# Two decoder layers on one core: twelve convolution taps as diagonal matmuls, and the low halves of the memory keys and values taken from PSUM

## The chip, the cores and the metric

The kernel runs on one core of a Trainium2 chip. The metric is device time in microseconds (us) of one execution. The five engines are TensorE (PE), VectorE (DVE), ScalarE (ACT), GpSimd (POOL) and SyncE (SP, which issues DMAs here). Each works through its own list of instructions in order and waits at semaphores for the others.

## The reference, cut to what matters

One inference step of a trunk of two layers, for 512 prompt positions and 8 sample positions, width 1024. Layer 0 mixes with an S5 and an HGRN2 branch, layer 1 with a Conformer convolution; each layer then has cross-attention into 256 memory tokens and a gated feed-forward part.

```
def _causal_dwconv(u, buf, w, b):
    n_tap = w.shape[0]
    ext = jnp.concatenate([buf.astype(u.dtype), u], axis=1)
    out = lax.conv_general_dilated(ext, w.astype(u.dtype)[:, None, :], (1,), 'VALID',
                                   dimension_numbers=('NWC', 'WIO', 'NWC'),
                                   feature_group_count=u.shape[-1])
    return out + b.astype(u.dtype), ext[:, ext.shape[1] - (n_tap - 1):]
...
def _conformer_conv(z, buf, w_dw, b_dw, ln_g, ln_b):
    a, gate = jnp.split(z, 2, axis=-1)
    u = a * jax.nn.sigmoid(gate)
    c, new_buf = _causal_dwconv(u, buf, w_dw, b_dw)
    return jax.nn.silu(_layer_norm(c, ln_g, ln_b)), new_buf
...
def _cross_attn(h, k, v, wq, wo):
    n, l, _ = h.shape
    q = (h @ wq).reshape(n, l, X_HEADS, X_HEAD_DIM)
    s = jnp.einsum('nlhd,nmhd->nhlm', q, k.astype(q.dtype)).astype(jnp.float32) * (X_HEAD_DIM ** -0.5)
```

The convolution has 31 taps on 1024 channels. The keys and values of the prompt's memory (`mem @ w_xk`, `mem @ w_xv`) are outputs too, for each layer.

## The kernel before, in words

Channels lie on the 128 partitions (eight channel tiles), positions along the free dimension: 512 prompt positions (`LP`) and 8 sample ones, in all 520 (`NT`). Norms and projections take the positions in two halves of 256 and 264 columns. A float32 product is made of three matmuls: each operand is split into a high half, rounded by ACT (`whi`, `xnh`, `Kh`, `Vh`), and a low half, the difference, which DVE or POOL subtracts (`wlo`, `xnl`, `Kl`, `Vl`).

The order of each engine's list is set when the kernel is built: a scheduler with a model of time (`schedule_with_timeline_sim`) places the instructions of each engine, and tiles come from pools with a fixed number of buffers. A tile that takes over a buffer waits for all readers of the tile before it there. Two such pools lie in PSUM: psA with three buffers of two banks (`pa`) and psB with two of one bank (`pb`). Weight tiles `wraw` have a ring of three, loaded by DMAs that SP issues.

Memory, layer 0 (`memory_k`, `memory_v`, called while the mixer's output is normed and added to the residual): four groups of 48 matmuls write the keys of two channel tiles each, `pkk`, a tile of psB. `kf` is a copy of it by ACT into SBUF, for the output's DMA; `Kh` is the rounded copy of `kf`, `Kl = kf - Kh`. The values, `pvv`, lie in psA and go the same way through `vf`. On ACT and DVE these stand among the work of the residual and the next norm: `x` adds (line 384), `xnh`, `xnl`, `whi`, `wlo`.

Layer 1 (`mixer1`): per channel tile the gate `cu` is made of two projections (`pca`, `pcg`), then the convolution runs tile by tile (`conv`). `POOL_TAPS` gives the taps that POOL does: ACT scales a shifted copy `ct`, POOL adds it to `cc`; tiles 1 and 4 lie wholly there, and of tile 6 fifteen taps. The other taps are `scalar_tensor_tensor` operations of DVE, in place on a PSUM tile `pcv` of psB, which ACT starts with tap 0 and the bias. The generator `chain` hands out DVE's taps, `CSTEP` (13) of them with each gate. Then `memory_k` and `memory_v` of layer 1 follow, with plain float32 matmuls (lines 1262 and 1293) and `pkk` and `pvv` both in psA, and the LayerNorm's column sums `pcs` over the eight `cc` tiles.

Of the kernel before, what the change touches and what calls it, by code (L numbers as in the profile page):

```python
# [9 lines left out]
F32 = mybir.dt.float32  # L10
F32R = mybir.dt.float32r
I32 = mybir.dt.int32
AF = mybir.ActivationFunctionType
# [5 lines left out]
P = 128  # L19
D = 1024  # L20
KC = D // P
LP = 512
NB = 8
NT = LP + NB
# [16 lines left out]
CPAIR = (1, 3)  # L41
NE = "VG"
LG = ((0, 0, 0), (0, 0, 0), (0, 1, 1))
POOL_TAPS = {1: 31, 4: 31, 6: 15}
CSTEP = 13
FILL = (4, 1, 5, 4)
NSOP = 8
START = (0, (0, 2, 0), 1, (2, 2, 0), (4, 4, 0), 2, (0, 4, 1), (4, 4, 1))
# [7 lines left out]
NM = 256  # L56
# [3 lines left out]
CW = 31  # L60
# [12 lines left out]
def _cols(n):  # L73
    a = _col[0]
    _col[0] += n
    return a
# [8 lines left out]
PC_CB = _cols(KC)  # L85
# [16 lines left out]
def trunk(ctx, tc, I, O, dbg=None):  # L102
    nc = tc.nc
    V, A, G, T = nc.vector, nc.scalar, nc.gpsimd, nc.tensor
# [21 lines left out]
    def pb(name):  # L126
        return psB.tile([P, 512], F32, tag="pb", name=name)

    def act(out, in_, f, **kw):
        return A.activation(out, in_, f, **kw)  # L130
# [5 lines left out]
    def tt(e, out, a, b, op):  # L136
        e.tensor_tensor(out, a, b, op=op)  # L137

    def stt(out, in0, s, in1, op0, op1):
        V.scalar_tensor_tensor(out, in0, s, in1, op0=op0, op1=op1)  # L140
# [7 lines left out]
    MUL, ADD, SUB = ALU.mult, ALU.add, ALU.subtract  # L148

    def f32(t):  # L150
        return t.bitcast(F32)
# [3 lines left out]
    ident = cst[:, 0:128]  # L155
# [14 lines left out]
    def pcol(base, c):  # L170
        return par[:, base + c:base + c + 1]
# [237 lines left out]
    def mixer0(nxt):  # L409
# [28 lines left out]
        with ExitStack() as es:  # L438
# [296 lines left out]
            def s5_emit(hf, Hs, E, other):  # L735
                Y = sop([P, 16, H5], "Y")
                for gq in range(2):
# [3 lines left out]
                    for g4 in range(4):  # L741
# [6 lines left out]
                        for g2 in range(2):  # L748
                            g = 2 * j + g2
                            T.matmul(pv[:, g2, g4, :], TPt[hf][:, g].rearrange("p c t -> p (c t)"), Us[hf, g][:, NB:U5],  # L750
                                     start=False, stop=True)
                        for _ in range(FILL[3] // 2):
                            next(other)
# [97 lines left out]
            in_u(mm(pa("pu"), load_w(I["w_ab_in"][3]), xs))  # L851
            fill(FILL[0])
            s5_u(0)
            s5_u(1)
            M = []
            for hf in range(2):
                M.append(s5_ops(hf))
                s5_rows(hf)
                fill(0 if hf else FILL[1])
            for hf in range(2):  # L860
# [4 lines left out]
            E = [s5_E(hf) for hf in range(2)]  # L865
            fill(FILL[2])
            Hsts, t1, t2 = s5_scan()
# [216 lines left out]
    def mixer1(bd, nxt, kvp, hs, mem):  # L1084
        nrm, xs = bd.nrm, bd.nrm.xs
        l = 1
        with ExitStack() as es:
            cf = es.enter_context(tc.tile_pool(name="cf", bufs=1))
            cw = par[:, PC_CW:PC_CW + CW * KC].rearrange("p (c j) -> p c j", j=CW)

            us, cs = [], [None] * KC
# [14 lines left out]
            def conv(n):  # L1106
                u, np_ = us[n], POOL_TAPS.get(n, 0)
                c = cs[n] = cf.tile([P, NT], F32, tag="cc", name="cc", bufs=KC)
# [13 lines left out]
                if cut:  # L1122
# [11 lines left out]
                        act(c[:, 0:1], pc[:, 0:1], AF.Copy)  # L1134
                    yield

            def chain(ns):
                for n in ns:
                    yield from conv(n)
# [2 lines left out]
            p0 = project_first(xs, bd.ws, RC, nrm, CUTC)  # L1142
            r = nrm.r
            gate(0, *p0[:2])
            dve = chain(n for n in range(KC) if POOL_TAPS.get(n, 0) < CW)
            for n in range(1, KC):
                for _ in range(CSTEP):
                    next(dve)
                pg = p0[2] if n == 1 else mm(pa("pcg"), wl(KC + n), xs)
                pu = mm(pa("pca"), wl(n), xs)  # L1150
                gate(n, pg, pu)
                if POOL_TAPS.get(n, 0) == CW:
                    for _ in conv(n):
                        pass
            for _ in dve:
                pass
            kmem = memory_k(1, mem, kvp)
            m = halves(slab("cmu"))
            rp, rs = slab("rstd"), slab("rs")
# [11 lines left out]
            for hv in range(2):  # L1171
                ps = column_sums([halves(c)[hv] for c in cs], hv, last)
                act(m[hv], ps, AF.Copy, scale=1.0 / D)
                for n in range(KC):
                    c = halves(cs[n])[hv]
# [12 lines left out]
            for hv in range(2):  # L1188
                for n in range(KC):
                    c = halves(cs[n])[hv]  # L1190
# [3 lines left out]
            kv = kmem, vals  # L1194
            ps = project_first(acts, [load_w(I["w_conf_out"][n]) for n in range(3)])
# [56 lines left out]
    def memory_k(l, m, kvp):  # L1252
        Kh, Kl = (kvp.tile([P, KC, NM], F32R, tag=t, name=t) for t in ("Kh", "Kl"))
        step = 4 if l == 1 else 2
        for n0 in range(0, KC, step):
            ps = pa("pkk") if l == 1 else pb("pkk")
            for n in range(n0, n0 + step):
                o = ps[:, (n - n0) * NM:(n - n0 + 1) * NM]
                if l == 1:
                    w = raw_w(I["w_xk"][l, n])  # L1260
                    for k in range(KC):
                        T.matmul(o, w[:, k], m[k], start=k == 0, stop=k == KC - 1)
                else:
                    wh, wl = load_w(I["w_xk"][l, n])
                    for k, (mh, ml) in enumerate(m):
                        for i, (a, b) in enumerate(((wh, mh), (wh, ml), (wl, mh))):
                            T.matmul(o, a[k], b, start=k == 0 and i == 0, stop=k == KC - 1 and i == 2)
                if n % 2 == 0:
                    continue
                kf = slab("kf", n=2 * NM)  # L1270
                ks = slice(n - 1, n + 1)
                kv = kf.rearrange("p (n m) -> p n m", n=2)
                act(kf, ps[:, (n - 1 - n0) * NM:(n + 1 - n0) * NM], AF.Copy)
                act(Kh[:, ks], kv, AF.Copy)
                tt(V, Kl[:, ks], kv, f32(Kh[:, ks]), SUB)
                nc.sync.dma_start(O["mem_k"][l, :, ks, :], kv)
        return Kh, Kl

    def memory_v(l, m, kvp, out):
        out += [kvp.tile([P, 2, D], F32R, tag=t, name=t) for t in ("Vh", "Vl")]  # L1280
        Vh, Vl = out
        for nh in range(2):
            ps = pa("pvv")
            for kp in range(4):
                src = I["w_xv"][l, nh, kp]
                ws = raw_w(src, nk=2, n=512) if l == 1 else load_w(src, nk=2, n=512)
                for k2 in range(2):
                    k = kp * 2 + k2
                    for mt_ in range(2):
                        ms = slice(mt_ * P, mt_ * P + P)  # L1290
                        o = ps[:, mt_ * 512:mt_ * 512 + 512]
                        if l == 1:
                            T.matmul(o, m[k][:, ms], ws[:, k2], start=k == 0, stop=k == KC - 1)
                            continue
                        (mh, ml), (wh, wl) = m[k], ws
                        for i, (a, b) in enumerate(((mh, wh), (ml, wh), (mh, wl))):
                            T.matmul(o, a[:, ms], b[k2], start=k == 0 and i == 0, stop=k == KC - 1 and i == 2)  # L1297
                if kp < 3:
                    yield
            for mt_ in range(2):  # L1300
                vf = slab("vf", n=512)
                cs_ = slice(nh * 512, nh * 512 + 512)
                act(vf, ps[:, mt_ * 512:mt_ * 512 + 512], AF.Copy)
                act(Vh[:, mt_, cs_], vf, AF.Copy)
                tt(V, Vl[:, mt_, cs_], vf, f32(Vh[:, mt_, cs_]), SUB)
                nc.sync.dma_start(O["mem_v"][l, mt_, :, cs_], vf)
            yield

# [270 lines left out]
    with tc.tile_pool(name="kv0", bufs=1) as kvp, tc.tile_pool(name="attn0", bufs=1) as ap:  # L1579
        kv = memory_k(0, mem, kvp), []  # L1580
# [4 lines left out]
    with tc.tile_pool(name="chs", bufs=1) as hp:  # L1585
# [10 lines left out]
        with tc.tile_pool(name="kv1", bufs=1) as kvp:  # L1596
            kv = mixer1(b3, b4, kvp, chs, mem)
# [121 lines left out]
```

## Time and profile before

| | us |
|---|---|
| median of 3 runs | 1747.28 (1746.36 to 1750.38) |
| the profiled execution | 1747.93 |
| its span, first to last instruction | 1746.2 |
| PE busy | 1641.7 (94%) |
| DVE busy | 994.1 (57%) |
| ACT busy | 805.7 (46%) |
| POOL busy | 653.4 (37%) |
| mean granted TensorE clock | 0.968 |

The span lies inside the execution's own time; 1.7 us are outside it. Busy shares are means over stages with different limits, so each stage has to be read for itself: the timelines give each engine's instructions in the order of time, with the idle time ahead of one and the instruction that ended it, and the busy time by stretch gives all engines side by side, with the granted clock as a share of full speed. Lines are those of the kernel before.

### The profile page before, as it was taken

The page shows a single profiled execution, that of the slowest core. Times are in us where ns is not written, and L with a number is a line of the kernel's source. Part 1 is how long each engine was busy: PE and PEld are TensorE (multiplying, and loading weights), DVE is VectorE, ACT ScalarE, POOL GpSimd, SP SyncE. Part 2 cuts the span into 40 slices and gives each one's busy share as a digit, 9 for nine tenths or more (in the row PEclk, how much of TensorE's full clock was granted, in tenths as well). Part 3 has the DMA queues.
Part 4 walks back from the last instruction along what each step waited for, and adds up shares of the span by engine and source line. Part 5 has one row for each costly group of instructions (what it writes and reads, how often), then busy time and mean ns, then how long its engine had stood idle before and what let it go on. Part 6 is the DMA issues. An engine that isn't in the chain of part 4 may idle for free.

```text
span 1746.2 us, 32833 instructions
## 1 busy us (share of the span) xinstructions
PE 1641.7 (94%) x13136; PEld 1546.8 (89%) x13136; DVE 994.1 (57%) x1814; ACT 805.7 (46%) x1599; POOL 653.4 (37%) x671
## 2 busy tenths in 40 slices
PE   8889899899898999999999996999998999999996
PEld 8889867888697999999998994698788999999996
DVE  8991686973548424424258999757346632323345
ACT  6342635672446434333346566664345533323343
POOL 2220150411026626152525899123004715334343
PEclk9988999999898999999999998999999999999998
DMA  7421521375641343332340324233651233232431
GB/s 237 131 61 46 175 76 49 115 237 180 241 148 50 96 123 93 88 97 75 108 125 24 108 78 145 90 117 121 203 190 61 82 88 99 77 114 65 120 88 50
DMA packets 77993, 195.21 MB, mean 112 GB/s; under 512 B 20720, under 2 KB 27728, under 8 KB 77712
## 3 DMA queue, kind: packets, MB, share of 16 engines
q1 hardware_dynamic: 77104, 190.75, 35.1%
q0 software_dynamic: 736, 2.36, 0.5%
q8 instruction: 103, 1.69, 0.4%
q14 instruction: 50, 0.41, 0.1%
HBM read 180.11 MB, written 12.96 MB: 111 GB/s over the span
## 4 chain that ended last, share of the span: by engine, by line
PE 68%; DVE 9%; issue 4%; ACT 2%; POOL 2%; DMA 1%; SPq 0%; POOLq 0%; DVEq 0%; ACTq 0%
PE pfb L203 14%; PE pfa L203 13%; PE pfo L203 12%; PE pt L203 4%; PE po L203 4%; PE pf L203 3%; PE pq L203 3%; PE pca L203 2%; POOL cc L137 2%; PE pcg L203 2%; DVE x L384 2%; PE pvo L1443 1%; PE psc L1409 1%; PE pvv L1297 1%; DVE y L377 1%
## 5 line engine op out<-in xcount | busy, mean ns | idle before, releaser
L130 ACT ACTIVATE whi<-wraw 128x512 fp32r<-128x512 f32 (+2 forms) x504 | 292.0, 588 | 557.2 <-PE pfo L203 131.2
L137 POOL TENSOR_TENSOR wlo<-wraw,whi 128x512 fp32r<-128x512 f32 x198 | 260.4, 1320 | 318.8 <-ACT whi L130 317.4
L137 DVE TENSOR_TENSOR wlo<-wraw,whi 128x512 fp32r<-128x512 f32 (+2 forms) x306 | 191.0, 634 | 174.4 <-ACT whi L130 167.2
L203 PE MATMUL pfb<-xnh,wlo 128*128 128x256 f32 (+1 forms) x672 | 135.8, 283 | 0.0
L203 PE MATMUL pfb<-xnl,whi 128*128 128x256 f32 (+1 forms) x672 | 135.1, 282 | 0.0
L203 PE MATMUL pfb<-xnh,whi 128*128 128x256 f32 (+1 forms) x672 | 135.1, 282 | 0.0
L203 PE MATMUL pfa<-xnh,wlo 128*128 128x256 f32 (+1 forms) x640 | 129.4, 283 | 0.0
L203 PE MATMUL pfa<-xnl,whi 128*128 128x256 f32 (+1 forms) x640 | 128.7, 282 | 0.0
L203 PE MATMUL pfa<-xnh,whi 128*128 128x256 f32 (+1 forms) x640 | 128.6, 282 | 0.0
L203 PE MATMUL pfo<-hlo,whi 128*128 128x256 f32 x604 | 122.0, 282 | 0.0
L203 PE MATMUL pfo<-hhi,wlo 128*128 128x256 f32 x604 | 121.4, 282 | 0.0
L203 PE MATMUL pfo<-hhi,whi 128*128 128x256 f32 x604 | 120.8, 282 | 0.0
L140 DVE SCALAR_TENSOR_TENSOR pcv<-cu,par,pcv 128x491 f32<-128x491 f32 (+19 forms) x160 | 109.5, 733 | 4.8 <-ACT pcv L130 3.4
L203 PE MATMUL pf<-xnl,whi 128*128 128x256 f32 (+1 forms) x288 | 86.5, 310 | 19.8 <-DVE xnl L140 19.8
L203 PEld LDWEIGHTS pfb<-xnh,whi 128*128 128x128 f32 x672 | 104.2, 188 | 0.0
L203 PEld LDWEIGHTS pfb<-xnl,whi 128*128 128x128 f32 x672 | 104.2, 188 | 0.0
L203 PEld LDWEIGHTS pfb<-xnh,wlo 128*128 128x128 f32 x672 | 104.2, 189 | 0.0
L203 PEld LDWEIGHTS pfa<-xnh,whi 128*128 128x128 f32 x640 | 99.3, 188 | 0.0
L203 PEld LDWEIGHTS pfa<-xnh,wlo 128*128 128x128 f32 x640 | 99.2, 189 | 0.0
L203 PEld LDWEIGHTS pfa<-xnl,whi 128*128 128x128 f32 x640 | 99.2, 188 | 0.0
L137 DVE TENSOR_TENSOR fa<-pfa,rstd 128x520 f32<-128x520 f32 x40 | 28.0, 699 | 125.1 <-PE pfa L203 125.0
L137 POOL TENSOR_TENSOR cc<-cc,ct 128x493 f32<-128x493 f32 (+15 forms) x74 | 94.1, 1276 | 4.9 <-ACT ct L130 1.1
(450 smaller groups left out, 4516.4 us busy)
## 6 DMA issues: line engine op xcount, KB each, us to landing
wraw<-w_ffn_in SPq DMA_DIRECT2D x88, 512.0 KB, 3.5
ck<-cK SPq DMA_DIRECT2D x32, 512.0 KB, 4.1
cv<-cV SPq DMA_DIRECT2D x32, 512.0 KB, 4.4
wraw<-w_ffn_out SPq DMA_DIRECT2D x32, 384.0 KB, 3.2
wraw<-w_ab_in SPq DMA_DIRECT2D x20, 512.0 KB, 3.7
wraw<-w_ffn_out SPq DMA_DIRECT2D x32, 320.0 KB, 2.9
wraw<-w_xk SPq DMA_DIRECT2D x16, 512.0 KB, 3.6
wraw<-w_xv SPq DMA_DIRECT2D x16, 512.0 KB, 4.1
```

What stands on the lines that cost most here:

```text
L130: return A.activation(out, in_, f, **kw)
L137: e.tensor_tensor(out, a, b, op=op)
L140: V.scalar_tensor_tensor(out, in0, s, in1, op0=op0, op1=op1)
L203: T.matmul(ps[:, o:o + m], a[k], b[hv], start=first and k == 0 and i == 0, stop=last and k == n - 1 and i == 2)
L377: i = f(*args)
L384: ordered(lambda: V.tensor_tensor(x[c][:, cs], x[c][:, cs], ys[c][:, cs], op=ADD))
L1297: T.matmul(o, a[:, ms], b[k2], start=k == 0 and i == 0, stop=k == KC - 1 and i == 2)
L1409: T.matmul(ps[:, h * NM:(h + 1) * NM], a[:, ls], b[:, 2 * h + dc, :], start=dc == 0 and i == 0, stop=dc == 1 and i == 2)
L1443: T.matmul(ps[:, o:o + 256], a[:, mt_, cs_], b[:, 2 * h + mt_, :], start=mt_ == 0 and i == 0, stop=mt_ == 1 and i == 2)
```

## The change

It has two parts. (1) In the convolution, channel tile 7 leaves the DVE chain: `conv_pe` lets PE compute its taps 1 to 12, each a matmul of `cu` with a 128x128 diagonal matrix `dg` that ACT scales from the identity (four buffers), summed in the `pcv` tile; ACT makes tap 0 and the bias directly in `cc`, DVE adds taps 13 to 30 to the PSUM tile, and one DVE addition puts `pcv` onto `cc`. POOL does 13 taps of tile 6 in place of 15, DVE the other two more. (2) In `memory_k` and `memory_v`, of both layers, `Kh` (`Vh`) is made from the PSUM tile, `Kl` (`Vl`) subtracts from it, and the copy `kf` (`vf`) for the output comes last.

```
--- before.py
+++ after.py
@@ -41,8 +41,9 @@
 CPAIR = (1, 3)
 NE = "VG"
 LG = ((0, 0, 0), (0, 0, 0), (0, 1, 1))
-POOL_TAPS = {1: 31, 4: 31, 6: 15}
+POOL_TAPS = {1: 31, 4: 31, 6: 13}
 CSTEP = 13
+PE_TAPS = {7: 12}
 FILL = (4, 1, 5, 4)
 NSOP = 8
 START = (0, (0, 2, 0), 1, (2, 2, 0), (4, 4, 0), 2, (0, 4, 1), (4, 4, 1))
@@ -1134,6 +1135,27 @@
                         act(c[:, 0:1], pc[:, 0:1], AF.Copy)
                     yield
 
+            def conv_pe(n):
+                u, k = us[n], PE_TAPS[n]
+                c = cs[n] = cf.tile([P, NT], F32, tag="cc", name="cc", bufs=KC)
+                act(c[:, LP:], u[:, LP:], AF.Identity, scale=tap(n, 0), bias=pcol(PC_CB, n))
+                tt(G, c[:, LP:], c[:, LP:], hs[:, n, :], ADD)
+                act(c[:, :LP], u[:, :LP], AF.Identity, scale=tap(n, 0), bias=pcol(PC_CB, n))
+                pc = pb("pcv")
+                for d in range(1, k + 1):
+                    dg = cf.tile([P, P], F32, tag="dg", name="dg", bufs=4)
+                    act(dg, ident, AF.Copy, scale=tap(n, d))
+                    T.matmul(pc[:, d:], dg, u[:, 0:LP - d], start=d == 1, stop=d == k)
+
+                def rest():
+                    for d in range(k + 1, CW):
+                        stt(pc[:, d:], u[:, 0:LP - d], tap(n, d), pc[:, d:], MUL, ADD)
+                        yield
+                    tt(V, c[:, 1:LP], c[:, 1:LP], pc[:, 1:], ADD)
+                    yield
+
+                return rest()
+
             def chain(ns):
                 for n in ns:
                     yield from conv(n)
@@ -1142,7 +1164,7 @@
             p0 = project_first(xs, bd.ws, RC, nrm, CUTC)
             r = nrm.r
             gate(0, *p0[:2])
-            dve = chain(n for n in range(KC) if POOL_TAPS.get(n, 0) < CW)
+            dve = chain(n for n in range(KC) if POOL_TAPS.get(n, 0) < CW and n not in PE_TAPS)
             for n in range(1, KC):
                 for _ in range(CSTEP):
                     next(dve)
@@ -1152,8 +1174,12 @@
                 if POOL_TAPS.get(n, 0) == CW:
                     for _ in conv(n):
                         pass
+            late = [conv_pe(n) for n in PE_TAPS]
             for _ in dve:
                 pass
+            for g in late:
+                for _ in g:
+                    pass
             kmem = memory_k(1, mem, kvp)
             m = halves(slab("cmu"))
             rp, rs = slab("rstd"), slab("rs")
@@ -1270,9 +1296,10 @@
                 kf = slab("kf", n=2 * NM)
                 ks = slice(n - 1, n + 1)
                 kv = kf.rearrange("p (n m) -> p n m", n=2)
-                act(kf, ps[:, (n - 1 - n0) * NM:(n + 1 - n0) * NM], AF.Copy)
-                act(Kh[:, ks], kv, AF.Copy)
-                tt(V, Kl[:, ks], kv, f32(Kh[:, ks]), SUB)
+                pk = ps[:, (n - 1 - n0) * NM:(n + 1 - n0) * NM]
+                act(Kh[:, ks], pk.rearrange("p (n m) -> p n m", n=2), AF.Copy)
+                tt(V, Kl[:, ks], pk.rearrange("p (n m) -> p n m", n=2), f32(Kh[:, ks]), SUB)
+                act(kf, pk, AF.Copy)
                 nc.sync.dma_start(O["mem_k"][l, :, ks, :], kv)
         return Kh, Kl
 
@@ -1300,9 +1327,10 @@
             for mt_ in range(2):
                 vf = slab("vf", n=512)
                 cs_ = slice(nh * 512, nh * 512 + 512)
-                act(vf, ps[:, mt_ * 512:mt_ * 512 + 512], AF.Copy)
-                act(Vh[:, mt_, cs_], vf, AF.Copy)
-                tt(V, Vl[:, mt_, cs_], vf, f32(Vh[:, mt_, cs_]), SUB)
+                pv = ps[:, mt_ * 512:mt_ * 512 + 512]
+                act(Vh[:, mt_, cs_], pv, AF.Copy)
+                tt(V, Vl[:, mt_, cs_], pv, f32(Vh[:, mt_, cs_]), SUB)
+                act(vf, pv, AF.Copy)
                 nc.sync.dma_start(O["mem_v"][l, mt_, :, cs_], vf)
             yield
 
```

The scheduler places all of it anew. In what follows, lines of the changed kernel stand one higher in the helpers (130 becomes 131, 137 becomes 138) and 26 or more behind `conv_pe`.

ACT, at the first two key groups of layer 0 (`pkk_3847` and `pkk_3921`; `xnh_3799` and those numbered behind it are the second half's high halves of the norm), before:

```order
L130 ACTIVATE whi_4002<-wraw_3996 128x512
L130 ACTIVATE kf_3916<-pkk_3847 128x512
L130 ACTIVATE xnh_3720<-x_78,par_76 128x256
L130 ACTIVATE whi_4032<-wraw_4030 128x512
L130 ACTIVATE whi_4036<-wraw_4030 128x512
L130 ACTIVATE whi_4072<-wraw_4070 128x512
L130 ACTIVATE xnh_3799<-x_78,par_76 128x264
L130 ACTIVATE xnh_3805<-x_78,par_76 128x264
L130 ACTIVATE whi_4076<-wraw_4070 128x512
L130 ACTIVATE kf_3990<-pkk_3921 128x512
L130 ACTIVATE whi_4106<-wraw_4104 128x512
```

and in the changed kernel:

```order
L131 ACTIVATE xnh_3799<-x_78,par_76 128x264
L131 ACTIVATE whi_4076<-wraw_4070 128x512
L131 ACTIVATE xnh_3805<-x_78,par_76 128x264
L131 ACTIVATE xnh_3811<-x_78,par_76 128x264
L131 ACTIVATE xnh_3817<-x_78,par_76 128x264
L131 ACTIVATE xnh_3822<-x_78,par_76 128x264
L131 ACTIVATE Kh_3845<-pkk_3847 128x512
L131 ACTIVATE Kh_3845<-pkk_3921 128x512
L131 ACTIVATE xnh_3826<-x_78,par_76 128x264
L131 ACTIVATE kf_3916<-pkk_3847 128x512
L131 ACTIVATE xnh_3830<-x_78,par_76 128x264
L131 ACTIVATE kf_3990<-pkk_3921 128x512
```

The copy `kf_3916` stood ahead of the second half's `xnh`, behind `whi_4002`; it now stands behind five of them, both `Kh` and a sixth.

DVE, at the end of the convolution, before (the last taps of tile 6, the add that joins its two parts, the last taps of tile 7):

```order
L140 SCALAR_TENSOR_TENSOR pcv<-cu,par,pcv 128x492
L140 SCALAR_TENSOR_TENSOR pcv<-cu,par,pcv 128x491
L137 TENSOR_TENSOR cc<-cc,pcv 128x512
L140 SCALAR_TENSOR_TENSOR pcv<-cu,par,pcv 128x490
L140 SCALAR_TENSOR_TENSOR pcv<-cu,par,pcv 128x489
```

and in the changed kernel (its last taps are those of tile 6):

```order
L141 SCALAR_TENSOR_TENSOR pcv<-cu,par,pcv 128x496
L141 SCALAR_TENSOR_TENSOR pcv<-cu,par,pcv 128x495
L141 SCALAR_TENSOR_TENSOR pcv<-cu,par,pcv 128x511
L138 TENSOR_TENSOR Vl<-pvv,Vh 128x512
L138 TENSOR_TENSOR cc<-cc,pcv 128x512
L138 TENSOR_TENSOR Vl<-pvv,Vh 128x512
L138 TENSOR_TENSOR cc<-cc,cmu 128x256 x8
```

A `Vl` now stands between the last tap and the last add of the convolution, and another behind it.

PE, from the end of the gate's projections to the LayerNorm's sums, before:

```order
L203 MATMUL pca<-xnh,wlo 128x264
L1262 MATMUL pkk<-mem,wraw 128x256 x64
L1293 MATMUL pvv<-wraw,mem 128x512 x16
L231 MATMUL pcs<-cc,cst 128x256 x8
L231 MATMUL pcs<-cc,cst 128x264 x8
```

and in the changed kernel:

```order
L1288 MATMUL pkk<-mem,wraw 128x256 x8
L1148 MATMUL pcv<-cu,dg 128x502
L1148 MATMUL pcv<-cu,dg 128x501
L1148 MATMUL pcv<-cu,dg 128x500
L1288 MATMUL pkk<-mem,wraw 128x256 x24
L1320 MATMUL pvv<-wraw,mem 128x512 x4
L1288 MATMUL pkk<-mem,wraw 128x256 x16
L1320 MATMUL pvv<-wraw,mem 128x512 x8
L232 MATMUL pcs<-cc,cst 128x256 x5
L1320 MATMUL pvv<-wraw,mem 128x512 x4
L232 MATMUL pcs<-cc,cst 128x256 x3
L232 MATMUL pcs<-cc,cst 128x264 x8
```

The twelve `pcv` matmuls (nine of them stand ahead of these rows, among the first 16 key matmuls) lie among the keys, and twelve of the value matmuls ahead of the first column sums, four more between them.

## Rows read from the trace of the kernel before

**Rows 1.** The page: busy time by engine; the chain that ended last.

```profile
PE 1641.7 (94%) x13136; PEld 1546.8 (89%) x13136; DVE 994.1 (57%) x1814; ACT 805.7 (46%) x1599; POOL 653.4 (37%) x671
...
PE 68%; DVE 9%; issue 4%; ACT 2%; POOL 2%; DMA 1%; SPq 0%; POOLq 0%; DVEq 0%; ACTq 0%
```

**Rows 2.** Busy by stretch: start:end, length, five engines (instructions), granted clock, DMA share, GB/s.

```profile
339.60:345.40 5.80, 5.78 (x48) 5.78 (x49) 5.80 (x9) 3.27 (x6) 4.42 (x5) 1.00 0.74 220
345.40:357.00 11.60, 11.60 (x99) 11.60 (x98) 11.60 (x23) 7.50 (x16) 3.90 (x8) 1.00 0.55 164
357.00:380.00 23.00, 23.00 (x105) 18.80 (x104) 15.34 (x26) 14.41 (x28) 0.00 (x0) 1.00 0.87 289
```

**Rows 3.** Timeline of PE: start, length, engine, line, operation, count, [idle before <-releaser].

```profile
87.17 0.80 PE L203 MATMUL ph<-xnh,whi 128*128 128x256 f32 x2 [5.67 <-ACT Ws L130]
...
339.62 0.39 PE L1267 MATMUL pkk<-mh,whi 128*128 128x256 f32 x1 [2.37 <-DVE rs L140]
...
345.42 0.28 PE L1267 MATMUL pkk<-mh,whi 128*128 128x256 f32 x1
```

**Rows 4.** Timeline of ACT, layer 0, 339 to 355 us.

```profile
339.99 0.58 ACT L130 ACTIVATE kf<-pkk 128x512 f32<-128x512 f32 x1
...
346.71 0.52 ACT L130 ACTIVATE xnh<-x,par 128x264 fp32r<-128x264 f32 x1 [2.00 <-DVE x L384]
...
354.06 0.50 ACT L130 ACTIVATE xnh<-x,par 128x264 fp32r<-128x264 f32 x1
354.47 1.14 ACT L130 ACTIVATE Kh<-kf 128x512 fp32r<-128x512 f32 x2
```

**Rows 5.** Timeline of DVE, layer 0, 350 to 356 us.

```profile
350.61 0.42 DVE L384 TENSOR_TENSOR x<-x,part 128x264 f32<-128x264 f32 x1
...
352.57 0.41 DVE L384 TENSOR_TENSOR x<-x,part 128x264 f32<-128x264 f32 x1
...
355.33 1.27 DVE L137 TENSOR_TENSOR Kl<-kf,Kh 128x512 fp32r<-128x512 f32 x2
```

**Rows 6.** Waits of PE from 395 to 560 us: total, times, longest.

```profile
PE pss L1347 <- DMA ck<-cK: 3.0, 3, 1.8
```

**Rows 7.** Busy by stretch, for the granted clock (columns: rows 2).

```profile
85.40:92.20 6.80, 5.03 (x23) 5.03 (x24) 6.41 (x14) 4.34 (x12) 0.00 (x0) 0.50 0.04 11
...
123.20:143.00 19.80, 19.67 (x96) 17.99 (x97) 8.63 (x15) 1.61 (x4) 8.41 (x1) 0.50 0.11 34
...
1097.00:1101.00 4.00, 2.52 (x7) 1.53 (x7) 3.47 (x5) 0.17 (x1) 0.00 (x0) 0.73 0.00 0
```

**Rows 8.** Busy by stretch, layer 1, convolution (columns: rows 2).

```profile
1034.00:1077.00 43.00, 41.62 (x161) 29.96 (x159) 40.60 (x61) 28.04 (x45) 40.88 (x34) 1.00 0.52 160
```

**Rows 9.** Timeline of PE, layer 1, 1073 to 1100 us.

```profile
1073.75 3.60 PE L1293 MATMUL pvv<-wraw,mem 128*128 128x512 f32 x8
1093.13 6.25 PE L231 MATMUL pcs<-cc,cst 128*128 128x256 f32 x14 [15.79 <-DVE cc L137]
```

**Rows 10.** Timeline of DVE, layer 1, 1036 to 1101 us.

```profile
1036.02 0.69 DVE L137 TENSOR_TENSOR cu<-cu,pcg 128x520 f32<-128x520 f32 x1
1036.62 5.87 DVE L140 SCALAR_TENSOR_TENSOR pcv<-cu,par,pcv 128x506 f32<-128x506 f32 x9
1042.40 1.62 DVE L137 TENSOR_TENSOR Kl<-kf,Kh 128x512 fp32r<-128x512 f32 x1
...
1067.01 0.68 DVE L137 TENSOR_TENSOR Kl<-kf,Kh 128x512 fp32r<-128x512 f32 x1
...
1074.28 6.25 DVE L140 SCALAR_TENSOR_TENSOR pcv<-cu,par,pcv 128x510 f32<-128x510 f32 x8 [2.11 <-ACT pcv L130]
...
1099.87 0.75 DVE L140 SCALAR_TENSOR_TENSOR cc<-cu,par,pcv 128x511 f32<-128x511 f32 x1
```

**Rows 11.** Groups by line, 1034 to 1101 us: busy, mean ns | idle.

```profile
L137 DVE TENSOR_TENSOR Kl<-kf,Kh 128x512 fp32r<-128x512 f32 x4 | 4.1, 1013 | 0.0
...
L137 DVE TENSOR_TENSOR Vl<-vf,Vh 128x512 fp32r<-128x512 f32 x2 | 2.6, 1281 | 0.0
```

## The prediction

> **What bounds the kernel now.** I read the page first: TensorE (PE) is busy 94% of the span and carries 68% of the chain that ended last, VectorE (DVE) 9% [rows 1]. So an edit counts where it makes PE wait, or shortens one of the few stretches in which PE waits for another engine. The change touches two places, and I looked at each on its own: the memory keys and values of layer 0, and the depthwise convolution of layer 1 with the keys and values beside it.
>
> In layer 0 the busy time by stretch shows a PE without a gap from 339.6 us on: 5.78 of 5.80, 11.60 of 11.60, 23.00 of 23.00 us [rows 2]. Its timeline shows that the second group of 48 key matmuls starts at 339.62 after 2.37 us of idle, and the third at 345.42, with no wait [rows 3]. In layer 1 the same view is the reverse: from 1034 to 1077 DVE is busy 40.60 and GpSimd (POOL) 40.88 of 43 us [rows 8], and PE then sits idle for 15.79 us until 1093.13 because of a DVE result [rows 9]. The DVE timeline runs from the last product of the gate at 1036.02 to the last tap at 1099.87 with one gap above half a microsecond, 2.11 us [rows 10]: there DVE is the bound.
>
> **Layer 0, the term that decides.** psB has two buffers, so the third group of keys takes the bank of the first, and PE's first matmul of that group needs every reader of the bank to be done. Before, the only reader was the copy `kf`, on ScalarE (ACT) at 339.99 for 0.58 us [rows 4], long before 345.42. `Kh` and `Kl` read `kf` from SBUF and could come as late as they liked: at 354.47 and 355.33 [rows 4, 5]. Now the readers are `Kh`, `Kl` and last `kf`, and the order of the instructions puts `Kh` about where it stood: behind the fifth `xnh` of the second half. That `xnh` needs the fifth `x` add, on DVE at 352.57 for 0.41 us [rows 5]. Step by step: one low-half subtraction fewer stands ahead of that add (about 0.6 us of pitch between DVE starts), so it ends at 352.98 - 0.6 = 352.4. The `xnh` takes 0.50 (352.9), `Kh` 0.57, half of the 1.14 for two (353.5), `Kl` 0.69, the price that DVE shows for one operand in PSUM [rows 10] (354.2), and `kf`, for which ACT is free by then, 0.58 (354.8). The third group starts near 354.9 instead of 345.42: **+9.5 us**. PE takes its work in order and has nothing else in front of it; behind it, it is busy without a gap [rows 2], so nothing gives the time back there. Bounds: 7 us if ACT gets to `Kh` two adds earlier (the fourth add is at 350.61 [rows 5]), 10.5 us if the low-half work stays ahead and both `Kl` come before `kf`. The last keys and all values follow with more room: their banks are wanted a whole group later.
>
> What the stall gives back: later in layer 0 PE waits 3.0 us for `cK` loads [rows 6]. Most of them start when PE frees a buffer, so they move with PE. I take 0.5 us, between 0 and 3.0.
>
> **The clock.** After PE waited 5.67 us the granted clock stood at 0.50 from 85.4 to 92.2 us, 5.0 us beyond the restart at 87.17 [rows 3, 7]; after 15.79 us it was 0.73 over 1097 to 1101, so half until about 1099.2, 6.1 us beyond the restart [rows 7, 9]. After 2.37 us it stayed at 1.00 [rows 2, 3]. [...] Ends: 0 (as after 2.37), and 9.9, half of the 19.8 us at 0.50 that one stretch shows [rows 7]; there 96 matmuls took 19.8 us, here 48 take 5.8, which is nearer to the first case.
>
> **Layer 1, the convolution.** From the last gate product at 1036.02 to the end of the last tap (1099.87 + 0.75) DVE needs 64.6 us [rows 10]. Nine taps from 1036.62 to 1042.40, on two channel tiles in turn, take 0.64 us each; eight on one tile from 1074.28 on take 6.25 us, 0.78 each, since each waits for the one before [rows 10]. The new DVE order, in the same stretch: the gate product 0.6; seven taps of tile 3 alone, 5.4; a wait for the next PSUM bank, 2.1 as now [rows 10]; 14 taps of tile 5 alone, 10.8; 35 of tiles 5, 7 and the first of 6 in turn, 22.4; the add of tile 7, 0.6; 16 of tile 6 alone, 12.4; four `Kl` and one `Vl` at 0.6 each, 3.0, and the final add 0.7. That is 58.0, and **6.6 us less**. Over 3 us of it come from the subtractions: four `Kl` and two `Vl` with both operands in SBUF took 6.7 us here [rows 11], one of them 1.62 and another 0.68, while the gate product, with one operand in PSUM, took 0.69 [rows 10]; and the second `Vl` now comes behind the final add.
>
> Against this stand three new waits on DVE. Tile 7's first DVE tap waits for the twelfth diagonal matmul; tile 6's bank comes free only when tile 5 is done; and the first `Vl` now stands ahead of the final add, so the end of the convolution also hangs on PE's values and on their weight loads. Each costs between 0 and the 2.1 us of the one such wait that the rows show; at 0.9 each, 2.7. So the LayerNorm starts 4 us earlier. Of this I give back 1 us (between 0 and 2) behind it, where two `Vl` and the later `vf` copies now stand between the low halves that PE waits for. **Net -3 us**, between 0 and -6.6.
>
> At nothing I cost PE's twelve matmuls: four value matmuls show as 8 records in 3.60 us, two to a matmul [rows 9], so twelve of that width take 10.8 us, under the 15.79 that PE idles there. The twelve diagonal weights of 128 columns take ACT at most the 0.50 us of its 264-column row [rows 4] each, 6 in all; ACT was busy 28.04 of 43 us [rows 8]. POOL does two taps less, and what it adds to tile 6 is wanted only by the final add. If that cover is gone, DVE waits for POOL or ACT, and this is bounded with the new waits above.
>
> [...]
>
> **The sum.** The profiled execution took 1747.9 us, 0.65 above the median of the runs shown (1747.3). 1747.9 + 9.5 + 2.5 - 0.5 - 3.0 = 1756.4, so **1756 us**, 0.5% slower; 0.2%, or 3.5 us, is about what a measurement of this kernel can tell from no change. Its own range: 1751 to 1762.
>
> **Rivals.** (a) The stall does not happen: the evacuation of a bank is `Kh`, `Kl` and `kf`, some 1.8 us by the rows above, and one group of matmuls takes 5.8 us [rows 3], so if ACT and DVE reach them while the other bank fills, PE never waits and only layer 1 counts: 1747.9 - 3 to - 6.6, 1741 to 1745, **faster**. It decides at a `kf` of the first group that ends before 345.4. For it: ACT had nothing to do for 2.00 us ahead of 346.71 [rows 4]. Against it: the engines take their work in order, and the rows put `Kh` behind an add of 352.57. [...] Chance 0.12. (b) The stall is at its low end, the clock does not fall and layer 1 gains its full 6.6: 1747.9 + 7 - 0.5 - 6.6 = 1747.8, no change that can be told. Chance 0.10. (c) Layer 1 gives nothing, because its end now hangs on PE's values and their loads: 1747.9 + 9.5 + 2.5 - 0.5 = 1759.4. For it: the first `Vl` stands right ahead of the last add. Chance 0.13. (d) The clock stays down for as long as in the 19.8 us stretch: 1763.8. Chance 0.05.
>
> **How the numbers follow.** The forecast has 0.60, and (c) and (d) are slower too: slower 0.78, same 0.10, faster 0.12. The range of 1746 to 1762 takes in the forecast's own, (b) and (c), and leaves out (a) and (d), 0.17.
>
> **What would show it.** Right: PE idle 8 to 10 us ahead of the third group of layer-0 keys, ended by `kf`; a granted clock of 0.50 for some 5 us behind it; in layer 1 the last convolution add some 4 us sooner after the last `cu`, and `Kl` at 0.7 us beside POOL. Wrong: a third group that starts within 2 us of the second's end, which would leave rival (a); a clock at 1.00 behind a long stall; or a DVE wait ahead of `Vl` that eats the layer-1 gain.

## The result, and the profile after

The changed kernel takes 1755.11 us (median of 14 runs, 1749.78 to 1759.25), the kernel before 1742.24 in the same comparison (14 runs, 1736.96 to 1750.38). The ratio is **1.0059, 95% interval [1.0042, 1.0076]**: slower by some 10 us, with 7 to 13 in the interval. The forecast was 1756 us, 0.5% slower. The execution of before on which the prediction's sum rests was one of the longer ones, 1747.9 us, so the difference has to be compared and not the time alone: 8.5 us forecast against those 10. The profiled execution of the changed kernel has a span of 1754.8 us.

First the place on which the forecast hung, the waits of TensorE (PE) in the profile of the changed kernel, 300 to 420 us (waiter, releaser: total, times, longest):

```profile
PE pkk L1293 <- ACT kf L131: 9.2, 1, 9.2
PE pkk L1293 <- DVE rs L141: 2.4, 1, 2.4
```

and PE's timeline there, where [rows 3] had the third key group start with no wait:

```profile
338.38 0.39 PE L1293 MATMUL pkk<-mh,whi 128*128 128x256 f32 x1 [2.36 <-DVE rs L141]
...
353.59 0.58 PE L1293 MATMUL pkk<-mh,whi 128*128 128x256 f32 x1 [9.24 <-ACT kf L131]
```

From the start of the second group to that of the third it took 5.80 us before and takes 15.21 now, 9.41 more. ScalarE (ACT) and VectorE (DVE) show why. The timeline of ACT in the changed kernel, where [rows 4] had `kf` at 339.99:

```profile
351.13 0.52 ACT L131 ACTIVATE xnh<-x,par 128x264 fp32r<-128x264 f32 x1 [0.23 <-DVE x L385]
351.55 1.06 ACT L131 ACTIVATE Kh<-pkk 128x512 fp32r<-128x512 f32 x2
352.50 0.51 ACT L131 ACTIVATE xnh<-x,par 128x264 fp32r<-128x264 f32 x1
352.94 0.60 ACT L131 ACTIVATE kf<-pkk 128x512 f32<-128x512 f32 x1
```

and of DVE, which answers to [rows 5]:

```profile
350.68 0.42 DVE L385 TENSOR_TENSOR x<-x,part 128x264 f32<-128x264 f32 x1
...
352.23 1.27 DVE L138 TENSOR_TENSOR Kl<-pkk,Kh 128x512 fp32r<-128x512 f32 x2
```

The fifth residual add ends at 351.10, its `xnh` follows, then both `Kh`, one more `xnh`, and `kf`, which ends at 353.54; PE starts at 353.59. `Kl` runs beside them on DVE, and ACT goes from one to the next without a wait for it. The busy time by stretch (columns as in [rows 2]) shows the clock behind it:

```profile
344.20:353.50 9.30, 0.14 (x2) 0.00 (x0) 9.30 (x20) 4.95 (x11) 3.80 (x8) 0.67 0.43 134
353.50:358.00 4.50, 4.41 (x22) 4.41 (x23) 2.08 (x5) 1.96 (x5) 0.00 (x0) 0.55 0.82 308
358.00:365.00 7.00, 7.00 (x61) 7.00 (x61) 3.58 (x6) 4.19 (x7) 0.00 (x0) 1.00 0.42 120
```

The granted clock is 0.55 over the 4.5 us behind the restart: 22 matmuls, where the full clock does 39 (61 in 7.00 us). The value matmuls then start at 366.8 us in place of 356.8; from the second group's start that is 28.4 us against 17.2 before, so **11.2 us** for stall and clock, 9.4 of it the stall.

In layer 1 the DVE timeline answers to [rows 10]:

```profile
1042.73 0.69 DVE L138 TENSOR_TENSOR cu<-cu,pcg 128x520 f32<-128x520 f32 x1
...
1050.58 2.33 DVE L141 SCALAR_TENSOR_TENSOR pcv<-cu,par,pcv 128x510 f32<-128x510 f32 x3 [1.93 <-ACT pcv L131]
...
1085.73 0.75 DVE L141 SCALAR_TENSOR_TENSOR pcv<-cu,par,pcv 128x510 f32<-128x510 f32 x1 [0.68 <-ACT pcv L131]
...
1089.64 0.69 DVE L138 TENSOR_TENSOR Kl<-pkk,Kh 128x512 fp32r<-128x512 f32 x1 [1.11 <-ACT Kh L131]
...
1102.10 0.69 DVE L138 TENSOR_TENSOR Vl<-pvv,Vh 128x512 fp32r<-128x512 f32 x1 [0.97 <-ACT Vh L131]
1102.70 0.68 DVE L138 TENSOR_TENSOR cc<-cc,pcv 128x512 f32<-128x512 f32 x1
```

From the last gate product to the end of the last add it takes 60.65 us, 4 less than the 64.6 of before. The row groups, 1040 to 1104 us, show the subtractions, where [rows 11] had 1013 ns each:

```profile
L138 DVE TENSOR_TENSOR Kl<-pkk,Kh 128x512 fp32r<-128x512 f32 x4 | 2.7, 685 | 1.1 <-ACT Kh L131 1.1
```

And PE has a wait that [rows 9] did not have, in its timeline (the last row is from SyncE's timeline, the issue of that weight's load):

```profile
1061.82 10.52 PE L1288 MATMUL pkk<-mem,wraw 128*128 128x256 f32 x48
1076.67 5.40 PE L1320 MATMUL pvv<-wraw,mem 128*128 128x512 f32 x8 [4.33 <-DMA wraw<-w_xv]
1081.90 7.07 PE L1288 MATMUL pkk<-mem,wraw 128*128 128x256 f32 x32
...
1072.37 0.33 SPq L176 DMA_DIRECT2D wraw<-w_xv  x1
```

### The profile page after: what moved, and what is told of

Read it like the earlier page. It is cut to its first block, busy times and chain, and to the rows that moved or that the text cites. A ratio compares the mean times of both kernels' runs of the same rounds, so it can differ in the third digit from the quotient of the medians.

```text
span 1754.8 us, 32891 instructions
## 1 busy us (share of the span) xinstructions
PE 1652.0 (94%) x13160; PEld 1552.6 (88%) x13160; DVE 988.2 (56%) x1805; ACT 809.5 (46%) x1608; POOL 647.7 (37%) x669
## 4 chain that ended last, share of the span: by engine, by line
PE 71%; DVE 7%; issue 3%; ACT 2%; DMA 2%; POOL 0%; SPq 0%; DVEq 0%; ACTq 0%; POOLq 0%
PE pfb L204 14%; PE pfa L204 13%; PE pfo L204 12%; PE pt L204 4%; PE po L204 4%; PE pf L204 4%; PE pq L204 3%; PE pca L204 2%; PE pcg L204 2%; DVE x L385 2%; PE pkk L1288 2%; PE psc L1437 1%; PE pvv L1324 1%; PE pcs L232 1%; PE pvv L1320 1%
## 5 line engine op out<-in xcount | busy, mean ns | idle before, releaser
L141 DVE SCALAR_TENSOR_TENSOR pcv<-cu,par,pcv 128x497 f32<-128x497 f32 (+22 forms) x151 | 104.5, 734 | 5.7 <-ACT pcv L131 3.9
L204 PEld LDWEIGHTS pfo<-hhi,whi 128*128 128x128 f32 x604 | 93.6, 188 | 0.0
```

Source lines behind the costliest of these rows:

```text
L204: T.matmul(ps[:, o:o + m], a[k], b[hv], start=first and k == 0 and i == 0, stop=last and k == n - 1 and i == 2)
```

## The experiments

Each kernel was timed against the kernel before in the same session. The table has the ratio, and three readings of the profiled execution: PE's idle time ahead of a key group of layer 0 (beyond the 2.4 us of before), and in layer 1 the time from the last gate product to the first column mean (`cmu`) and from there to the program's end. Each of the three comes from a single execution. The kernel before and the run with layer 0 alone, whose code is the same in layer 1, have 65.6 and 66.0 in the first of these two times, which DVE bounds [rows 10]; the second holds 645 us of other work, and the same two have 644.5 and 646.3.

| kernel | ratio to before, 95% | layer-0 wait | to `cmu` | `cmu` to end |
|---|---|---|---|---|
| before | 1 | 0 | 65.6 | 644.5 |
| changed | 1.0059 [1.0042, 1.0076] | 9.2 | 62.4 | 649.7 |
| e1, layer 0 as before | 1.0029 [1.0008, 1.0049] | 0 | 65.9 | 650.7 |
| e2, new order in layer 0 alone | 1.0054 [1.0028, 1.0080] | 9.3 | 66.0 | 646.3 |
| e3, convolution alone | 1.0004 [0.9987, 1.0021] | 0 | 63.0 | 649.5 |
| e4, new order in layer 1 alone | 1.0018 [1.0000, 1.0035] | 0 | 66.5 | 650.1 |
| e5, keys in psA | 1.0042 [1.0018, 1.0067] | 7.2 | 63.0 | 648.5 |
| e10, copy first | 1.0076 [1.0047, 1.0104] | 8.6 | 61.9 | 648.5 |
| e6, as e4, stores moved | 1.0020 [1.0001, 1.0040] | 0 | 68.5 | 651.9 |
| e7, as e1, stores moved | 1.0032 [1.0011, 1.0053] | 0 | 65.4 | 653.2 |
| e8, as e1, values tied | 1.0005 [0.9981, 1.0030] | 0 | 60.7 | 650.7 |
| e9, as e4, values tied | 0.9992 [0.9969, 1.0015] | 0 | 62.9 | 647.0 |
| b1, 15 taps, convolution alone | 0.9988 [0.9969, 1.0007] | 0 | 59.3 | 646.1 |
| b2, as e8, 15 taps | 1.0003 [0.9982, 1.0025] | 0 | 63.7 | 649.5 |

**The parts apart (e1 to e4).** The edit of e1, in `memory_k` (and the same in `memory_v`), shortened:

```
+if l == 0:
+    act(kf, pk, AF.Copy); act(Kh[:, ks], kv, AF.Copy); tt(V, Kl[:, ks], kv, f32(Kh[:, ks]), SUB)
+else:
     act(Kh[:, ks], pk..., AF.Copy); tt(V, Kl[:, ks], pk..., f32(Kh[:, ks]), SUB); act(kf, pk, AF.Copy)
```

> The changed kernel with the keys and values of layer 0 handled as before (copy first, high and low half from the copy). Theory: the whole loss is the bank that the third key group of layer 0 waits for; without it that group starts within 0.5 us of the second group's end, the granted clock stays at 1.00 there, and 9.2 us of stall and some 2.5 us of clock are gone: 1739 to 1742 against a before of about 1742 (ratio 0.998 to 1.000). Rival: the loss comes from layer 1 (diagonal matmuls and the values that the last add now waits for): the time stays above before, ratio 1.003 or more, and the stall in layer 0 moves elsewhere.

The stall is gone, but the time is not that of before: 1.0029, above the theory's 1.000 and at the rival's mark. In e1, then, what is left of the change costs 1.4 to 8.5 us and is not the gain that I had put down. That is not quite the layer 1 of the changed kernel, though: the scheduler placed the lists anew, and with the same source for layer 1 both `Vl` now stand ahead of the last add, DVE waits 3.0 us for the last `Kh` where it waited 1.1, and the column mean comes at 65.9 us and not at 62.4.

e2 is the kernel before with the new lines under `if l == 0`:

> The kernel before with the new order of keys and values in layer 0 alone. Theory: TensorE idle 9 to 9.5 us ahead of the third key group, ended by the copy on ScalarE, some 5 us at half clock behind it; 10 to 12 us slower than before (ratio 1.006 to 1.007), slower than the whole change if layer 1 gains. Rival (layer 1 causes the loss): within 2 us of before.

As the theory had it: PE idle 9.3 us ahead of the third group, and 1.0054, some 9 us, a little under the 10 to 12 expected. Layer 0 alone makes almost the whole loss. The changed kernel lies 0.05% above it, 1 us, with some 5 us either way by the two intervals. The losses of e1 and e2 add to more than that of the whole change, 0.83% against 0.59%; their intervals allow for it.

e3 is the changed kernel with the old lines of `memory_k` and `memory_v` in both layers:

> The diagonal taps and the two taps taken from GpSimd alone, keys and values of both layers as before. Theory: no stall in layer 0; in layer 1 the subtractions with both operands in SBUF cost up to 1.6 us again, so from the last gate product to the first column mean some 1 to 4 us less than before and 1 to 2 more than in the changed kernel; 1 to 3 us faster than before (ratio 0.998 to 0.9995). Rival: the gain of layer 1 comes from the subtractions alone, and this is no faster than before or slower.

The column mean comes 2.6 us sooner, as expected, yet the time is that of before (1.0004), the rival's: what the stage gained is not there at the end.

e4 is the kernel before with the new lines under `if l == 1`:

> The kernel before with the new order of keys and values in layer 1 alone. Theory: each low half of layer 1 takes 0.7 us in place of up to 1.6, 2.5 us less on VectorE; the time lies between 2 us faster and 1 us slower than before (ratio 0.999 to 1.0005), since the order also moves. Rival: the values ahead of the last add, or a bank held longer in layer 1 too, cost more than that: 3 us or more slower.

1.0018, 3 us slower, with 0 to 6 in the interval: the rival's end. Its waits in the stage, PE's and then DVE's, show where the shorter subtractions went:

```profile
PE pvv L1299 <- DMA wraw<-w_xv: 4.5, 1, 4.5
PE pkk L1262 <- DMA wraw<-w_xk: 3.5, 1, 3.5
...
DVE Kl L137 <- ACT Kh L130: 4.5, 2, 3.5
```

Before, PE waited for no weights in this stretch and DVE for no `Kh`. Each `Kl` takes 0.69 us, and the 4.5 us that DVE waits ahead of them are more than the longer `Kl` of before had cost, 1.3 us for four at 1013 ns [rows 11].

**Which reader holds the bank (e10, e5).** In e10 the copy is first again in layer 0, with `Kh` and `Kl` still from PSUM:

```
+if l == 0: act(kf, pk, AF.Copy)
 act(Kh[:, ks], pk..., AF.Copy)
 tt(V, Kl[:, ks], pk..., f32(Kh[:, ks]), SUB)
-act(kf, pk, AF.Copy)
+if l != 0: act(kf, pk, AF.Copy)
```

> The changed kernel with the copy of the keys and values for the output made first again in layer 0, but high and low half still taken from PSUM. Theory (any reader that stands behind the second half's norm holds the bank): the third key group still waits, now for the low half of the first, 8 to 9 us, and the time stays within 2 us of the changed kernel, ratio to before 1.004 to 1.007. Rival (what matters is that the copy comes last): no wait above 1 us, ratio below 1.002.

The third group waits 8.62 us, and PE's timeline names the other reader:

```profile
349.45 0.58 PE L1293 MATMUL pkk<-mh,whi 128*128 128x256 f32 x1 [8.62 <-DVE Kl L138]
```

It is the new readers of the bank that cost, wherever the copy stands. The ratio, 1.0076, is a little above the 1.004 to 1.007 expected; its interval reaches down to 1.0047. e5 gives the keys of layer 0 the pool of three buffers:

```
-            ps = pa("pkk") if l == 1 else pb("pkk")
+            ps = pa("pkk")
```

> The changed kernel with the four key groups of layer 0 in the pool of three larger PSUM buffers in place of the pool of two. Theory (the third group waits for the first group's bank): the third group starts right behind the second, and the wait passes to the fourth group, which now takes over the first one's buffer: 3 to 8 us there, ended by the copy on ScalarE, so 2 to 6 us faster than the changed kernel (ratio to before 1.002 to 1.005). Rival (the PSUM reads or the moved instructions themselves delay the keys, whatever the buffer): the third group still waits some 9 us.

The third group is no longer held by a bank; it waits 0.72 us for a low half of a weight, and the fourth waits 7.18:

```profile
341.73 0.39 PE L1293 MATMUL pkk<-mh,wlo 128*128 128x256 f32 x1 [0.72 <-DVE wlo L138]
...
350.35 0.58 PE L1293 MATMUL pkk<-mh,whi 128*128 128x256 f32 x1 [7.18 <-ACT kf L131]
```

The wait goes where the buffer is taken over. With e1 and e2 that settles the cause in layer 0.

**What holds layer 1 back (e6 to e9).** My first theory, from e4's waits, was SyncE's queue: the stores of `kf` stand in it ahead of weight loads, and `kf` is later. e6 and e7 issue those stores, and those of `vf`, from ACT's queue:

```
-nc.sync.dma_start(O["mem_k"][l, :, ks, :], kv)
+(nc.scalar if l == 1 else nc.sync).dma_start(O["mem_k"][l, :, ks, :], kv)
```

> The new order of keys and values in layer 1 alone, and the stores of these keys and values issued from ScalarE's queue instead of SyncE's. In the run with layer 1 alone SyncE waited 7.5 us for the copies (2.1 before), TensorE 3.5 and 4.5 us for weights that SyncE issues behind those stores, and VectorE 4.5 us for the high halves. Theory (the stores of the later copies hold back the weight loads): TensorE's waits for these weights fall to under 3 us together and VectorE's for the high halves to under 2; 2 to 4 us faster than layer 1 alone, so about as before. Rival (the weight ring is freed late by TensorE itself, the queue is not what holds): the waits stay within 1 us of what they were, and so does the time.

> The changed kernel with layer 0 as before and the stores of layer 1's keys and values issued from ScalarE's queue. The run without that move had TensorE wait 4.1 us for value weights and VectorE 3.0 for a high half of the keys and 1.7 for one of the values, and came out 0.3% slower than before. Theory (the queue): those waits fall to half or less and the time to 0.999 to 1.001 of before. Rival (the ring): they stay, and the ratio stays near 1.003.

That theory fell. The same waits in e6:

```profile
PE pvv L1299 <- DMA wraw<-w_xv: 3.7, 1, 3.7
PE pkk L1262 <- DMA wraw<-w_xk: 3.6, 1, 3.6
...
DVE Kl L137 <- ACT Kh L130: 5.8, 2, 3.1
```

and the ratios stay at 1.0020 and 1.0032. The order of the instructions held the answer. By the kernel's lists, in the changed kernel SyncE loads the key weights `wraw_12366`, `12376`, `12391`, `12401` and then the first value weight `12430`, into a ring of three. PE uses `12376` for eight key matmuls, then `12430` for four value matmuls, and only then `12391` and `12401` for the last sixteen key matmuls.

So `12391` and `12401` lie in the ring unused, and the load of `12430` has to wait until PE is done with `12376`. The rows above agree: PE's key matmuls end at 1072.34, the load is issued at 1072.37, and PE stands idle for the whole load, 4.33 us, to 1076.67. The last 16 key matmuls, `Kh` and `Kl` come behind that. e8 and e9 tie the first value matmul behind the last key matmul:

```
-            last = []
+            last = list(last_key)        # the last key matmul, kept by memory_k
```

> The changed kernel with layer 0 as before, and the first value matmuls of layer 1 tied behind the last key matmul. In the changed kernel TensorE's order puts four of them ahead of the last 16 key matmuls, while SyncE loads all eight key weights first into a ring of three, so that the value weight is loaded only when the sixth key weight is used up. Theory (this order is what took the gain of layer 1): TensorE's wait of 4.1 us for value weights falls under 1.5, VectorE's waits for high halves (4.7 us in all) under 2, from the last gate product to the first column mean 61 to 63 us against 65.9 without the tie, and the time is 3 to 7 us below that run: ratio to before 0.997 to 1.001. Rival (layer 1 loses by the longer chain from PSUM itself): waits move but the time to the first column mean stays above 65 us, ratio near 1.003.

> The new order of keys and values in layer 1 alone, with the same tie. Without the tie TensorE waited 3.5 us for key weights and 4.5 for value weights, and VectorE 4.5 for high halves of the keys. Theory (order): those waits fall to under 4 us together on TensorE and under 2 on VectorE, the first column mean comes 2 us sooner, and the time is that of before within 2 us, or below it. Rival: 2 us or more slower than before, as without the tie.

PE's timeline in e8, where the value matmuls now follow the keys without a wait for their weights:

```profile
1048.12 10.52 PE L1290 MATMUL pkk<-mem,wraw 128*128 128x256 f32 x48
1061.67 7.17 PE L1290 MATMUL pkk<-mem,wraw 128*128 128x256 f32 x32 [3.02 <-ACT kf L131]
1068.68 10.46 PE L1328 MATMUL pvv<-wraw,mem 128*128 128x512 f32 x24
```

The column mean comes at 60.7 us in place of 65.9 (e8 against e1) and at 62.9 in place of 66.5 (e9 against e4), and the ratios fall by 0.24% and 0.26%, each to that of before. DVE's waits in the stage, e1 and then e8, where it has none for `Vh`:

```profile
DVE Kl L138 <- ACT Kh L131: 3.0, 1, 3.0
...
DVE Vl L138 <- ACT Vh L131: 1.7, 1, 1.7
```

```profile
DVE Kl L138 <- ACT Kh L131: 0.4, 1, 0.4
```

So the traces show what the order costs in the stage; in the time neither pair is apart beyond its intervals (e1 1.0008 to 1.0049, e8 0.9981 to 1.0030), though both moved the same way. PE still waits 3.0 us for `kf`, which may be why the scheduler had put values there. In e9 the wait for value weights is gone, that for key weights stays at 3.7 us, and DVE waits 2.0 us for `Kh` where it had waited 4.5.

**Toward a faster kernel (b1, b2).** b1 takes e3 with `PE_TAPS = {7: 15}` and `POOL_TAPS[6] = 15`; b2 takes e8 with the same two numbers.

> The diagonal taps alone, fifteen instead of twelve, GpSimd with its fifteen taps of tile 6 as before, keys and values of both layers as before. Theory (VectorE bounds the convolution, TensorE has 10 us or more to spare): five VectorE taps fewer than in the run with twelve and thirteen, 3 to 4 us less from the last gate product to the first column mean, so 3 to 6 us faster than before (ratio 0.9965 to 0.9985). Rival (the end of the convolution is set by GpSimd or TensorE, or what is gained there is waited for again at the cache loads of attention): within 2 us of before.

> The tied kernel (layer 0 as before, keys and values of layer 1 from PSUM) with fifteen diagonal taps and GpSimd's fifteen taps of tile 6. Theory (VectorE bounds the stage once the order is put right): five VectorE taps fewer than with twelve and thirteen, 3 to 4 us below the tied kernel, ratio to before 0.995 to 0.999. Rival (the sum then hangs on the values ahead of the last add): no faster than the run with fifteen taps and the copies first (0.9988).

b1 is the best of the stage, 6.3 us sooner at the column mean, and 0.9988 [0.9969, 1.0007]: faster than the changed kernel by the two intervals, than the kernel before not shown. The 3 to 6 us of its theory did not come; the time is its rival's. In b2 DVE waits 5.4 us for `Vh`, so the end hangs on PE's values, as its rival had it; no gain.

## Why the prediction was right

**The number.** Part of the agreement at 1756 us is luck: the sum starts from an execution 5.7 us above the median of before in the comparison. The fair measure is the difference, 8.5 us forecast against 10.3 by the ratio and 12.9 between the two medians. What was right is the way and the cause of the loss, the stall of layer 0.

**The stall.** Forecast 9.5 us; measured 9.2 idle, 9.4 from start to start, released by `kf`, and up to `Kh` in the order of events that was forecast. The last step was not as forecast: it let `kf` wait for `Kl` on DVE and took ACT to be free. In the rows `Kl` is not on the path; ACT is held by the second group's `Kh` and the sixth `xnh`, which the order of instructions had shown ahead of `kf`. That these take about as long as the `Kl` in their place is luck: the steps of 0.5, 0.57, 0.69 and 0.58 us add to 2.3, and from the end of the add to the end of `kf` it took 2.44. e1, e2, e5 and e10 confirm the cause, a bank held by readers behind the norm's work.

**The clock.** The sum has +2.5 us for it, and no run shows that term; what the changed kernel's profile shows in its place is 0.55 over 4.5 us, 22 matmuls where the full clock does 39, which loses about 2.0. Stall and clock together: 12.0 forecast, 11.2 measured.

**What the stall gives back.** Forecast 0.5 us from PE's waits for `cK`. Measured nothing: those waits are 3.2 us in the changed kernel against 3.0 [rows 6].

**Layer 1: the step that was not borne out.** The net of -3 us. Up to the last add the stage came out: that add ended 4.0 us sooner, counted from the last gate product, and the price of one operand in PSUM was 0.685 us. The new waits on DVE came to 2.8 us against 2.7, but not as named: 0.68 for tile 6's bank, 0.97 for `Vl`, none for tile 7's first tap, and 1.11 for a `Kh` that I had not named. In the time no run shows a gain of layer 1. The changed kernel (1.0059) is not below e2 (1.0054), which has none of the layer-1 edits, though their intervals leave room for 3 us; e1, with another order of the lists, is slower by 1.4 to 8.5 us; of its two halves the convolution is worth nothing in the time (e3), and the new order of keys and values costs 0 to 6 us (e4), where I had it as the source of half the gain.

Two things were missed. One is the order of PE's matmuls against the order of the weight loads: I named the values' weight loads as something that the last add would hang on, and priced that wait on DVE at 0.9 us, without seeing that the ring makes PE wait a whole load ahead of the last keys. e8 and e9 show in their stage that this order costs, 5.2 and 3.6 us at the column mean. The other is what I gave back behind the stage, 1 us. The mixer's output projection comes there, in the tiles `pf` and then `po`. The stretch from the first `pf` to the first `po`, before and in the changed kernel (columns as in [rows 2]):

```profile
1123.60:1142.90 19.30, 18.40 (x147) 17.61 (x146) 13.15 (x31) 16.00 (x35) 0.53 (x1) 1.00 0.63 237
```

```profile
1126.60:1147.90 21.30, 19.45 (x147) 17.85 (x146) 14.34 (x32) 17.37 (x36) 1.51 (x2) 1.00 0.63 216
```

The same number of matmuls takes 2 us longer, with 1.85 us of PE idle in place of 0.90, and 0.9 us of it is a wait for `czh`, the high halves of the norm's result, which ACT makes among the last `Vh` and `vf`; before, PE had no wait for `czh` there. From the column mean to the first `po` it takes 41.3 to 41.7 us in the four kernels with the old order of keys and values in layer 1 (before, e2, e3, b1) and 42.5 to 45.9 in the ten with the new one; the changed kernel loses 1.4 there.

Of the rivals, (a) is refuted: `kf` of the first group ended at 353.54, not before 345.4. The groups did rotate through two banks, and PE still waited 9.2 us; with three buffers (e5) the wait moved on to the fourth group, 7.2 us. (c), which let layer 1 gain nothing, comes closest to the ratio's difference: 11.5 us against 10.3, with 8.5 for the forecast; the interval of 7 to 13 us holds both, so the result alone does not tell them apart.

**The price from PSUM.** Forecast 0.69 us for a subtraction with one operand in PSUM; measured 685 ns, against 0.68 us for the shortest of before, with both in SBUF [rows 10]. The excess of before, a mean of 1013 ns [rows 11], is gone: the four `Kl` of the changed kernel take 0.68 or 0.69 us each, all beside a GpSimd that its timeline shows at work from 1046.45 to 1095.71. What made the excess is not shown. Before, GpSimd was at work from 1038.19 to 1092.35, and beside it two of the four `Kl` took 1.62 and 1.08 us and the other two 0.68.

What stays open: the column mean is 2.6 us sooner in e3 and 4.9 in e8, and their times are those of before. In the profiles it is used up behind the column mean, most of it in the second attention: from the first `po` to the first `psot` (the sample positions' attention output, transposed) it takes 137.8 us before, 141.0 in the changed kernel, 141.9 in e3 and 141.6 in e8, but 138.6 in b1 and 137.4 in e9. PE's waits for `cK` and `cV` loads go with it: in the same order 4.6, 6.4, 7.2, 6.8, 5.1 and 5.4 us. Why PE waits longer for these loads in some kernels is not shown, and with intervals of 0.2% the times can't say how much of the gain is lost there.

## What to carry to other kernels

When an operation is moved from a copy in SBUF to the PSUM tile itself, it becomes a reader of the bank, and the place of that reader in its engine's list sets when the next group of matmuls starts; a queue with other work ahead of it can cost far more than the operation (here 9.2 us for readers of 0.5 to 0.7 us each). Compare, for each ring of buffers, the order in which loads fill it with the order in which the engine empties it: a scheduler that moves four matmuls forward into a small gap can expose a whole load (here 4.33 us). And price a part of a change by what waits for it, even where its instructions get shorter.

## What the runs showed that I had not expected

One kernel's times spread, 1737 to 1750 us for before, and the profiles differ in a stretch of the program that no edit touched. After a wait of 4.8 us of PE in the first mixer the granted clock stays at half over 123 to 143 us in some profiled executions and soon returns in others. The same stretch in the profile of before, and in that of e3:

```profile
123.00:143.00 20.00, 19.67 (x96) 17.99 (x97) 8.83 (x16) 1.61 (x4) 8.61 (x1) 0.50 0.11 34
```

```profile
123.00:143.00 20.00, 17.88 (x141) 16.44 (x142) 11.88 (x22) 2.61 (x5) 10.20 (x1) 0.91 0.14 48
```

141 matmuls in place of 96 in the same 20 us: at the full clock's 0.12 us for one (48 in 5.78 us [rows 2]), those 45 are some 5 us by estimate. e3's last gate product came at 1028.6 us against 1036.0, and e8 and e9 have the higher clock there as well (0.87 and 0.94 over 118 to 145 us, where before has 0.62), e4 the lower (0.50 over 123 to 143). So the spans of single executions can differ by 5 us for a cause that has nothing to do with a change, and stages are better compared from a fixed event within each.
